# The output projection of a hybrid decoder layer as seven products of quarter matrices

## The chip, the core and the metric

The kernel runs on one core of a Trainium2 chip. The core has five engines, each with an instruction queue of its own that it works off in order: TensorE (PE) multiplies matrices, with weight loads (PEld) beside it; VectorE (DVE), ScalarE (ACT) and GpSimd (POOL) work elementwise; SyncE (SP) only starts transfers (DMA). The metric is device time in microseconds (us), the median of several runs of one program; the profile is of one more execution.

## What is computed

One layer: RMSNorm of `x`, one wide input projection, three branches (sparse attention `a`, sliding-window attention `b`, an RWKV-7 scan `c`), and then what matters here. Every array is float32; there are 1024 tokens of width 1024.

```python
y_a = y_a * jax.nn.silu(cols["a_z"])      # likewise y_b, y_c
gates = jax.nn.sigmoid(cols["merge"].reshape(b, t, N_BRANCHES, d) + b_merge[l])
mixed = (gates[:, :, 0] * (y_a @ proj_a[l])
         + gates[:, :, 1] * (y_b @ proj_b[l])
         + gates[:, :, 2] * (y_c @ proj_c[l]))
x = x + mixed @ w_out[l]
return rms_norm(x, final_g)
```

## The kernel before, in words

Every float32 matrix is split into a high part that the matmul takes without loss and a low remainder, so that a product costs three matmuls (`mm3`): high by high, high by low, low by high. A stationary operand of 128x128 is loaded, and 512 columns stream past it.

The program up to `finish` is the same before and after. `finish` has two stages.

**The product stage.** For branch 2, then 1, then 0 (`br`), and for each pair `m2` of the eight blocks of 128 output columns, the weights of the branch projection are loaded (`wr`) and split (`wh`, `wl`), the merge gates `g` are loaded from DRAM scratch, and four tiles of PSUM (`pp`, four buffers) are filled, each 128x512. A tile costs 6 matmuls in branches 2 and 1, and 12 in branch 0. DVE reads a tile out of PSUM and multiplies it by its gate: into `mixed` for branch 2, into a temporary `t` (three buffers) for the others, which POOL then adds to `mixed` (in the last step DVE does). In the text, branch 0's sixteen tiles are numbered 1 to 16 in their order; a tile can only be begun when the tile four before it has been read. The branch inputs `y` are loaded and split by `gated` a step or more ahead; the eight row blocks of `w_out` are loaded (`wor`) and split (`o_hi` by ACT, `o_lo` by DVE) in between, as the table `WO` says.

**The output stage.** For each of eight blocks `b` of 128 tokens: load `x`, split the block of `mixed` (`mh`, `ml`), two PSUM tiles `op` of 128x512 with 24 matmuls each (the last block's second tile is cut in two of 256 columns, each in a PSUM tile of its own), add to `x`, square and sum (ACT), multiply by `final_g` (POOL), scale by the root mean square, store.

Instructions are written in program order and a list scheduler then decides the order of each engine's queue, also of SP's; buffers are handed out from free ones. No engine looks past the head of its queue.

Of the kernel before, what the change touches and what calls it, by code (L numbers as in the profile page):

```python
# [1140 lines left out]
def finish(tc, a, out, eps, split_w, mm3, wst, y_scr, o_scr, z_scr, g_scr):  # L1141
    nc = tc.nc
    pe, act, dve, pool = nc.tensor, nc.scalar, nc.vector, nc.gpsimd
    KB = ((0, 4), (4, 2), (6, 2))

    GF, GL = (6, 7), {(2, 0): (4,), (2, 2): (5,), (2, 4): (0,), (2, 6): (1,), (1, 0): (2,), (1, 2): (3,)}
    HB_, GB, YB, TT_, OB = 5, 4, 14, 3, 1
    WO = {(1, 2): (4,), (1, 6): (5,), (0, 0): (6, 7), (0, 2): (0, 1), (0, 4): (2, 3)}
    with ExitStack() as st:
        wo = st.enter_context(tc.tile_pool(name="wo", bufs=1, side="right"))  # L1150
        mxp = st.enter_context(tc.tile_pool(name="mx", bufs=1, side="right"))
        mixed = mxp.tile([P, KT, T], F32, name="mixed")
# [4 lines left out]
        wk = yp = st.enter_context(tc.tile_pool(name="yy", bufs=YB))

        def parts(names, shape, first):

            return [(hp if first else yp).tile(shape, F32R, name=n, tag="ya" if first else "yy") for n in names]

        with tc.tile_pool(name="pp", bufs=4, space=PSUM) as pp:
# [22 lines left out]
            o_hi, o_lo = {}, {}  # L1186
            for br in (2, 1, 0):
                i0, n = KB[br]
                for m2 in range(0, 8, 2):
# [4 lines left out]
                    for h in range(2):
                        nc.sync.dma_start(gs[h], g_scr[br][m2 // 2][:, :, h * NH:(h + 1) * NH].rearrange("m p t -> p m t"))
                    for i in GL.get((br, m2), ()):
                        ys[i] = gated(i)
                    for k in WO.get((br, m2), ()):

                        if k < 4:  # L1200
                            o_hi[k], o_lo[k] = parts(("o_hi", "o_lo"), [P, D], k == 0)
                        else:
                            o_hi[k], o_lo[k] = [wo.tile([P, D], F32R, name=n, tag=f"wo{k}", bufs=2) for n in ("o_hi", "o_lo")]
                        raw = hp.tile([P, D], F32, name="wor", tag="wor", bufs=OB)
# [19 lines left out]
        nc.sync.dma_start(fg, a["final_g"].to_broadcast([P, D]))  # L1224
        for b in range(NB):
            bs = slice(b * P, (b + 1) * P)
            x = hp.tile([P, D], F32, name="x", tag="h", bufs=HB_)
            nc.sync.dma_start(x, a["x"][bs])
            sq = wk.tile([P, D], F32, name="sq", tag="g", bufs=GB)
            ss = wk.tile([P, 4], F32, name="ss", bufs=2)  # L1230
            mh, ml = [yp.tile([P, KT, P], F32R, name=n, tag="yy") for n in ("mh", "ml")]
            for ks in (slice(0, 6), slice(6, 8)):
                act.activation(mh[:, ks], mixed[:, ks, bs], AF.Copy, scale=0.5)
                dve.scalar_tensor_tensor(ml[:, ks], mixed[:, ks, bs], 0.5, mh[:, ks].bitcast(F32), op0=OP.mult,
                                         op1=OP.subtract)

            cuts = (0, 512, 768, 1024) if b == NB - 1 else (0, 512, 1024)
            for i, (n0, n1) in enumerate(zip(cuts, cuts[1:])):
                ns = slice(n0, n1)
                ps = po.tile([P, NH], F32, name="op")[:, 0:n1 - n0]  # L1240
                dense(mm3(ps, lambda k: (mh[:, k], ml[:, k]), lambda k: (o_hi[k][:, ns], o_lo[k][:, ns]), KT))
                dve.tensor_add(x[:, ns], x[:, ns], ps)
                act.activation(sq[:, ns], x[:, ns], AF.Square, accum_out=ss[:, i:i + 1])
                if i:
                    dve.tensor_add(ss[:, 0:1], ss[:, 0:1], ss[:, i:i + 1])
                pool.tensor_mul(x[:, ns], x[:, ns], fg[:, ns])
            act.activation(ss[:, 0:1], ss[:, 0:1], AF.Sqrt, bias=eps[:, 0:1], scale=1.0 / D)
            dve.reciprocal(ss[:, 0:1], ss[:, 0:1])
            act.activation(x[:, 0:NH], x[:, 0:NH], AF.Copy, scale=ss[:, 0:1])
            dve.tensor_scalar(x[:, NH:], x[:, NH:], ss[:, 0:1], None, op0=OP.mult)  # L1250
            nc.scalar.dma_start(out[bs, 0:NH], x[:, 0:NH])
            nc.sync.dma_start(out[bs, NH:], x[:, NH:])


# [43 lines left out]
```

## Time and profile before

| | us |
|---|---|
| median of three runs | 1163.83 |
| lowest and highest of them | 1160.35, 1166.82 |
| the profiled execution | 1166.12 |
| its span (first to last recorded instruction) | 1164.4 |

The span is what the rows below count in, from 0; the profiled execution's own time lies 1.7 us above its span, and 2.3 us above the median of the runs. PE is busy for 1127.4 us of the span, DVE for 732.6, ACT for 562.8 and POOL for 209.8. The product stage begins on PE at 980.1 us, branch 0 at 1027.1 us and the output stage at 1070.7 us.

### The profile page before, as it was taken

What the parts mean: (1) busy time and instruction counts of PE and PEld (TensorE: products, weight loads), DVE (VectorE), ACT (ScalarE), POOL (GpSimd) and SP (SyncE); (2) the same over time, 40 slices, a digit from 0 to 9 for tenths busy, and PEclk for the clock granted to TensorE, in tenths of its full rate; (3) what the DMA queues carried; (4) which work ended last, traced back from release to release, by engine and by line L of the source; (5) the groups of instructions that cost most, each with busy time, mean ns of one, the idle gap of its engine ahead of it and who ended that gap; (6) DMA issues with size and microseconds to landing.
All of it is one profiled execution on the core that took longest, in us unless ns stands there. A gap on an engine that the chain in (4) does not pass through costs nothing.

```text
span 1164.4 us, 18199 instructions
## 1 busy us (share of the span) xinstructions
PE 1127.4 (97%) x6838; PEld 925.2 (79%) x6838; DVE 732.6 (63%) x1468; ACT 562.8 (48%) x1311; POOL 209.8 (18%) x230
## 2 busy tenths in 40 slices
PE   6989999999999899989999999999999999999997
PEld 6868887678868898868778778887888778788886
DVE  6486725977337221794788787458878776676322
ACT  7544134724326222554677665457766654222322
POOL 1100000100013011181112111211111120373222
PEclk9989999999999999999999999999999999999999
DMA  6012411122402121111111111111111169882221
GB/s 236 17 42 65 118 60 37 55 91 82 124 20 82 67 93 37 46 49 55 48 47 41 51 50 47 45 55 42 48 48 42 41 226 308 277 286 79 73 73 55
DMA packets 61464, 97.73 MB, mean 84 GB/s; under 512 B 16192, under 2 KB 24768, under 8 KB 61120
## 3 DMA queue, kind: packets, MB, share of 16 engines
q1 hardware_dynamic: 59936, 94.31, 24.9%
q10 hardware_dynamic: 1440, 2.26, 0.5%
q8 instruction: 54, 0.88, 0.3%
q14 instruction: 34, 0.28, 0.1%
HBM read 69.81 MB, written 26.74 MB: 83 GB/s over the span
## 4 chain that ended last, share of the span: by engine, by line
PE 74%; DVE 12%; ACT 6%; DMA 5%; issue 2%; SPq 0%; POOLq 0%; POOL 0%; ACTq 0%; DVEq 0%
PE pj L214 12%; PE pj L218 12%; PE pj L216 12%; PE s L1035 4%; PE tr L877 3%; DVE p L1071 3%; PE op L216 2%; PE op L214 2%; PE op L218 2%; ACT p L1044 2%; PE pv L868 2%; PE pv L869 2%; PE pp L214 2%; PE pp L218 2%; PE pp L216 2%
## 5 line engine op out<-in xcount | busy, mean ns | idle before, releaser
L214 PE MATMUL pj<-x_hi,wh 128*128 128x512 f32 x768 | 306.6, 399 | 4.0 <-DVE xr L403 3.2
L218 PE MATMUL pj<-x_hi,wl 128*128 128x512 f32 x768 | 306.7, 400 | 1.4 <-DVE wl L197 1.4
L216 PE MATMUL pj<-x_lo,wh 128*128 128x512 f32 x768 | 306.7, 399 | 0.0
L214 PEld LDWEIGHTS pj<-x_hi,wh 128*128 128x128 f32 x768 | 145.6, 190 | 33.5 <-DVE xr L403 3.6
L218 PEld LDWEIGHTS pj<-x_hi,wl 128*128 128x128 f32 x768 | 145.7, 190 | 30.3 <-DVE wl L197 1.9
L216 PEld LDWEIGHTS pj<-x_lo,wh 128*128 128x128 f32 x768 | 145.6, 190 | 30.2 <-issue 1.9
L196 ACT ACTIVATE wh<-wr 128x512 fp32r<-128x512 f32 (+1 forms) x120 | 70.0, 600 | 119.2 <-PE pj L216 84.0
L1044 ACT ACTIVATE p<-s,nm 128x512 f32<-128x512 f32 (+3 forms) x160 | 93.4, 589 | 43.1 <-DVE nm L1041 23.6
L197 POOL TENSOR_TENSOR wl<-wr,wh 128x512 fp32r<-128x512 f32 x58 | 77.1, 1342 | 191.6 <-ACT wh L196 161.6
L881 DVE TENSOR_TENSOR tl<-tr,th 128x512 fp32r<-128x512 f32 x132 | 89.8, 684 | 19.5 <-ACT th L879 18.3
L879 ACT ACTIVATE th<-tr 128x512 fp32r<-128x512 f32 x132 | 78.7, 597 | 43.8 <-PE tr L877 42.1
L1041 DVE TENSOR_REDUCE nm<-s 128x1 f32<-128x512 f32 (+3 forms) x130 | 84.8, 660 | 22.2 <-PE s L850 18.3
L877 PE MATMUL tr<-ident,p 128*128 128x128 f32 x528 | 81.3, 275 | 4.7 <-DVE tl L881 3.5
L1035 PE MATMUL s<-k,q 128*128 128x512 f32 (+3 forms) x320 | 82.3, 354 | 0.2
L877 PEld LDWEIGHTS tr<-ident,p 128*128 128x128 f32 x528 | 62.8, 141 | 20.4 <-DVE tl L881 6.2
L197 DVE TENSOR_TENSOR wl<-wr,wh 128x512 fp32r<-128x512 f32 (+1 forms) x62 | 45.9, 749 | 47.0 <-ACT wh L196 43.3
L868 PE MATMUL pv<-th,V 128*128 128x512 f32 (+1 forms) x162 | 68.1, 426 | 2.5 <-DVE o L855 2.5
L1035 PEld LDWEIGHTS s<-k,q 128*128 128x128 f32 x320 | 54.2, 188 | 14.6 <-ACT p L1044 4.7
L1071 DVE TENSOR_SCALAR p<-p,nm 128x512 f32<-128x512 f32 (+3 forms) x160 | 62.8, 460 | 0.7
L869 PE MATMUL pv<-tl,V 128*128 128x512 f32 (+1 forms) x162 | 59.9, 376 | 0.0
L214 PE MATMUL pp<-y_hi,wh 128*128 128x512 f32 x128 | 50.3, 393 | 2.2 <-ACT wh L196 1.3
L216 PE MATMUL op<-o_lo,mh 128*128 128x512 f32 (+1 forms) x136 | 51.2, 377 | 0.0
(307 smaller groups left out, 2006.2 us busy)
## 6 DMA issues: line engine op xcount, KB each, us to landing
wr<-w SPq DMA_DIRECT2D x96, 256.0 KB, 2.8
g_scr<-gs SPq DMA_DIRECT2D x48, 256.0 KB, 2.0
g<-g_scr SPq DMA_DIRECT2D x24, 512.0 KB, 5.6
xr<-x SPq DMA_DIRECT2D x8, 512.0 KB, 5.5
z_scr<-gs SPq DMA_DIRECT2D x16, 256.0 KB, 2.2
wor<-w_out SPq DMA_DIRECT2D x8, 512.0 KB, 4.7
x<-x SPq DMA_DIRECT2D x8, 512.0 KB, 5.4
o_scr<-ol SPq DMA_DIRECT2D x24, 128.0 KB, 2.4
```

Of the source, the lines that this page charges most:

```text
L197: weng[0].tensor_sub(lo, raw, hi.bitcast(F32))
L214: pe.matmul(ps, lh, rh, start=k == 0, stop=False)
L216: pe.matmul(ps, lh, rl, start=False, stop=False)
L218: pe.matmul(ps, ll, rh, start=False, stop=k == n - 1)
L868: pe.matmul(pv, v.rearrange("p j d -> p (j d)"), th, start=start, stop=False, skip_group_check=True)
L869: pe.matmul(pv, v.rearrange("p j d -> p (j d)"), tl, start=False, stop=stop, skip_group_check=True)
L877: pe.transpose(tr[:, h], p4[h], ident)
L881: dve.tensor_sub(tl, tr, th.bitcast(F32))
L1035: pe.matmul(ps[:, i], q[h0 + i][:, qs], ks[j][:, kc:kc + n], start=i == 0 and j == 0, stop=wrap and j == 1, skip_group_check=True)
L1041: dve.tensor_reduce(nm[:, c, 0, hs], ps, axis=AX.X, op=OP.max, negate=True)
L1044: act.activation(weights(h, c), ps[:, i], AF.Exp, bias=nm[:, c, 0, h:h + 1], accum_out=nm[:, c, 1, h:h + 1])
L1071: eng.tensor_scalar(p, p, nm[:, c, 3, h:h + 1], None, op0=OP.mult)
```

## The change

The output projection becomes one level of Winograd's form of Strassen's method. `mixed` (tokens by inner dimension) and `w_out` (inner dimension by columns) are cut into 2x2 quarters A11..A22 and B11..B22 of 512x512. With S1 = A21+A22, S2 = S1-A11, S3 = A11-A21, S4 = A12-S2 and T1 = B12-B11, T2 = B22-T1, T3 = B22-B12, T4 = B21-T2, seven products replace eight: A11 B11, S1 T1, S2 T2, S4 B22, S3 T3, A12 B21, A22 T4. Two sets of four PSUM banks hold running sums: `op` (called u) takes A11 B11, then S2 T2, S3 T3 and A22 T4 on top, and is added to `x` after each; `pp` (called c) takes S1 T1 and S4 B22, and then A12 B21 anew.

The order of the loops is turned: products outside (`steps`), the four token blocks of a half inside. A unit is one product and one token block: 12 matmuls of 512 columns into one bank, and one add to half a row of `x` by DVE. All eight blocks of `x` stay on chip (five in the buffers `h`, three in `yy`). `rows` forms a unit's sum on POOL and splits it (ACT, DVE), three units ahead (`AHEAD`); `weigh` forms and splits one of four 128-row slices of a product's weights, in the step before the one that uses it, or for B11 and T1 inside branch 0; the four splits of A11 also stand inside branch 0 (at `m2 == 6` in the code). `done` squares, sums and scales what is final. The loads of quarters replace the loads of row blocks: B11 in branch 1, B12 and B22 in branch 0, B21 at the start of the output stage.

```diff
-    HB_, GB, YB, TT_, OB = 5, 4, 14, 3, 1
-    WO = {(1, 2): (4,), (1, 6): (5,), (0, 0): (6, 7), (0, 2): (0, 1), (0, 4): (2, 3)}
+    HB_, GB, YB, TT_ = 5, 4, 14, 3
...
+        def load(name, j, n, first=False):
+            raws[name] = []
+            for c in range(2):
+                t = (hp if first else yp).tile([P, 2, NH], F32, name="wor", tag="wor" if first else "yy")
+                k = 4 * j + 2 * c
+                nc.sync.dma_start(t, a["w_out"][k:k + 2, :, n * NH:(n + 1) * NH].rearrange("k p n -> p k n"))
+                raws[name] += [t[:, i] for i in range(2)]
...
+        def weigh(name, k, minus=None, into=None):
...
+            hi, lo = ws[name]
+            t = raws[name][k]
+            if minus:
+                pool.tensor_sub(t, raws[minus[0]][k], raws[minus[1]][k])
+            act.activation(hi[:, k], t, AF.Copy)
+            dve.tensor_sub(lo[:, k], t, hi[:, k].bitcast(F32))
...
+        def rows(what, i):
...
+            if what == "S1":
+                pool.tensor_add(src, a21, a22)
+            elif what == "S2":
+                pool.tensor_sub(src, src, a11)
+            elif what == "S3":
+                pool.tensor_sub(src, a11, a21)
+            elif what == "S4":
+                pool.tensor_sub(src, a12, src)
...
+            act.activation(t[:, 0], src, AF.Copy, scale=0.5)
+            dve.scalar_tensor_tensor(t[:, 1], src, 0.5, t[:, 0].bitcast(F32), op0=OP.mult, op1=OP.subtract)
+            return t
...
-                    for k in WO.get((br, m2), ()):
...
-                        nc.sync.dma_start(raw, a["w_out"][k])
-                        for h in range(2):
-                            ns = slice(h * NH, (h + 1) * NH)
-                            act.activation(o_hi[k][:, ns], raw[:, ns], AF.Copy)
-                            dve.tensor_sub(o_lo[k][:, ns], raw[:, ns], o_hi[k][:, ns].bitcast(F32))
+                    if br == 1 and m2 == 6:
+                        load("B11", 0, 0, True)
+                    if br == 0 and m2 == 0:
+                        load("B12", 0, 1)
+                        for k in range(4):
+                            weigh("B11", k)
+                    if br == 0 and m2 == 4:
+                        load("B22", 1, 1)
+                        for k in range(4):
+                            weigh("T1", k, ("B12", "B11"), "B11")
+                    if br == 0 and m2 == 6:
+                        ahead = [rows("A11", i) for i in range(4)]
...
-        for b in range(NB):
...
-            cuts = (0, 512, 768, 1024) if b == NB - 1 else (0, 512, 1024)
...
-                ps = po.tile([P, NH], F32, name="op")[:, 0:n1 - n0]
-                dense(mm3(ps, lambda k: (mh[:, k], ml[:, k]), lambda k: (o_hi[k][:, ns], o_lo[k][:, ns]), KT))
...
+            steps = (("A11", "B11", "+u", 0, 0, False, None),
+                     ("S1", "T1", "+c", 1, 1, False, ("T2", ("B22", "T1"), "T1")),
+                     ("S2", "T2", "u", 0, 1, False, ("B22", None, None)),
+                     ("S4", "B22", "c", 0, 1, True, ("T3", ("B22", "B12"), "B12")),
+                     ("S3", "T3", "u", 1, 1, True, ("B21", None, None)),
+                     ("A12", "B21", "+c", 0, 0, True, ("T4", ("B21", "T2"), "T2")),
+                     ("A22", "T4", "u", 1, 0, True, None))
...
+                for c0, c1 in ((0, 256), (256, 512)) if at == len(todo) - 1 else ((0, 512),):
+                    for k in range(4):
+                        pe.matmul(ps[:, c0:c1], t[:, 0, k], hi[:, k, c0:c1], start=new and k == 0, stop=False,
+                                  skip_group_check=True)
...
+                    x, o = xs[4 * half + i], col_ * NH
+                    dve.tensor_add(x[:, o + c0:o + c1], x[:, o + c0:o + c1], ps[:, c0:c1])
+                    if full:
+                        done(4 * half + i, o + c0, o + c1)
```

Since the scheduler places `weigh` and `rows` by what is ready, their place in the queues is not that of the code. Three places follow; a name's number tells buffers apart.

**POOL in branch 0.** `mixed<-mixed,t` is the add of one tile of branch 0 (`t_10150` to `t_10260` are tiles 3 to 8 before; `t_10120` to `t_10198` are tiles 2 to 6 after). `wor_10019` and `wor_10021` hold the two halves of B11, then T1, then T2; `wor_10077` and `wor_10079` hold B12, then T3; `wor_10247` and `wor_10249` hold B22. Before:

```order
L1223 TENSOR_TENSOR mixed_9554<-mixed_9554,t_10150 128x512
L1223 TENSOR_TENSOR mixed_9554<-mixed_9554,t_10166 128x512
L1223 TENSOR_TENSOR mixed_9554<-mixed_9554,t_10212 128x512
L1223 TENSOR_TENSOR mixed_9554<-mixed_9554,t_10228 128x512
L1223 TENSOR_TENSOR mixed_9554<-mixed_9554,t_10244 128x512
L1223 TENSOR_TENSOR mixed_9554<-mixed_9554,t_10260 128x512
```

After:

```order
L1191 TENSOR_TENSOR wor_10021<-wor_10079,wor_10021 128x512 x2
L1278 TENSOR_TENSOR mixed_9554<-mixed_9554,t_10120 128x512
L1278 TENSOR_TENSOR mixed_9554<-mixed_9554,t_10136 128x512
L1278 TENSOR_TENSOR mixed_9554<-mixed_9554,t_10152 128x512
L1191 TENSOR_TENSOR wor_10019<-wor_10247,wor_10019 128x512 x2
L1191 TENSOR_TENSOR wor_10077<-wor_10247,wor_10077 128x512
L1278 TENSOR_TENSOR mixed_9554<-mixed_9554,t_10182 128x512
L1191 TENSOR_TENSOR wor_10021<-wor_10249,wor_10021 128x512 x2
L1191 TENSOR_TENSOR wor_10077<-wor_10247,wor_10077 128x512
L1191 TENSOR_TENSOR wor_10079<-wor_10249,wor_10079 128x512 x2
L1278 TENSOR_TENSOR mixed_9554<-mixed_9554,t_10198 128x512
```

Between the adds of tiles 4 and 6 there now stand eight subtractions, four that form T2 and four that form T3; the first rows are the second half of T1.

**DVE in branch 0.** `t<-g,pp` reads a tile out of PSUM (`t_10166` to `t_10260` are tiles 4 to 8 before; `t_10152` to `t_10230` are tiles 4 to 8 after), `wl` is the low part of projection weights, `o_lo` that of `w_out`, and `mh<-mixed,mh` the low part of A11's rows. Before:

```order
L1221 SCALAR_TENSOR_TENSOR t_10166<-g_10086,pp_10153 128x512
L1209 TENSOR_TENSOR o_lo_10192<-wor_10193,o_hi_10191 128x512
L197 TENSOR_TENSOR wl_10264<-wr_10265,wh_10263 128x512
L197 TENSOR_TENSOR wl_10264<-wr_10269,wh_10263 128x512
L1221 SCALAR_TENSOR_TENSOR t_10212<-g_10179,pp_10199 128x512
L1221 SCALAR_TENSOR_TENSOR t_10228<-g_10179,pp_10215 128x512
L1209 TENSOR_TENSOR o_lo_10278<-wor_10279,o_hi_10277 128x512 x2
L1221 SCALAR_TENSOR_TENSOR t_10244<-g_10180,pp_10231 128x512
L1221 SCALAR_TENSOR_TENSOR t_10260<-g_10180,pp_10247 128x512
```

After:

```order
L1276 SCALAR_TENSOR_TENSOR t_10152<-g_10074,pp_10139 128x512
L198 TENSOR_TENSOR wl_10234<-wr_10235,wh_10233 128x512
L198 TENSOR_TENSOR wl_10234<-wr_10239,wh_10233 128x512
L1276 SCALAR_TENSOR_TENSOR t_10182<-g_10165,pp_10169 128x512
L1276 SCALAR_TENSOR_TENSOR t_10198<-g_10165,pp_10185 128x512
L1216 SCALAR_TENSOR_TENSOR mh_10343<-mixed_9554,mh_10343 128x512
L1216 SCALAR_TENSOR_TENSOR mh_10346<-mixed_9554,mh_10346 128x512
L1276 SCALAR_TENSOR_TENSOR t_10214<-g_10166,pp_10201 128x512
L1216 SCALAR_TENSOR_TENSOR mh_10349<-mixed_9554,mh_10349 128x512
L1216 SCALAR_TENSOR_TENSOR mh_10352<-mixed_9554,mh_10352 128x512
L1276 SCALAR_TENSOR_TENSOR t_10230<-g_10166,pp_10217 128x512
```

Two of the four splits of A11 now stand ahead of the read of tile 7 and two ahead of that of tile 8; each waits for ACT's high part, which waits for POOL's add of tile 6. The splits of `w_out` that stood between these reads are gone from this place.

**SP in branch 0.** `wr_10171` to `wr_10269` are the projection weights of steps `m2` = 2 and 4 before, `wr_10157` to `wr_10239` the same after; `g` are gates. Before:

```order
L195 DMA wr_10171<-proj 128x512
L195 DMA wr_10175<-proj 128x512
L1195 DMA g_10179<-g_scr01_92 128x2x512
L1205 DMA wor_10185<-w_out 128x1024
L1195 DMA g_10180<-g_scr01_92 128x2x512
L195 DMA wr_10265<-proj 128x512
L195 DMA wr_10269<-proj 128x512
L1228 DMA x_10656<-x 128x1024
L1205 DMA wor_10193<-w_out 128x1024
```

After:

```order
L196 DMA wr_10157<-proj 128x512
L196 DMA wr_10161<-proj 128x512
L1250 DMA g_10165<-g_scr01_92 128x2x512
L1250 DMA g_10166<-g_scr01_92 128x2x512
L196 DMA wr_10235<-proj 128x512
L196 DMA wr_10239<-proj 128x512
L1250 DMA g_10243<-g_scr02_93 128x2x512
L1177 DMA wor_10247<-w_out 128x2x512
L1177 DMA wor_10249<-w_out 128x2x512
L1250 DMA g_10244<-g_scr02_93 128x2x512
```

The two loads of B22 (`wor_10247`, `wor_10249`) stand behind `wr_10239`, which waits until its buffer has been read: by DVE's second `wl_10156`, the low part of step 2's weights. In DVE's queue that subtraction follows two `o_lo_10252<-wor_10019,o_hi_10251`, the first two low parts of T1.

## Rows read from the trace of the kernel before

**Rows 1.** The page: the span, and section 1 (busy time, share of span, instructions).

```profile
span 1164.4 us, 18199 instructions
PE 1127.4 (97%) x6838; PEld 925.2 (79%) x6838; DVE 732.6 (63%) x1468; ACT 562.8 (48%) x1311; POOL 209.8 (18%) x230
```

**Rows 2.** Stretches: start:end, length, busy (instructions) by engine, clock, DMA share, GB/s.

```profile
950.00:1000.00 50.00, 50.00 (x222) 41.30 (x222) 29.21 (x51) 19.32 (x37) 2.54 (x2) 1.00 0.84 280
1000.00:1050.00 50.00, 47.77 (x206) 38.03 (x206) 36.92 (x50) 11.69 (x23) 31.48 (x22) 1.00 0.85 279
1070.00:1158.00 88.00, 88.00 (x412) 73.83 (x411) 31.37 (x56) 26.95 (x61) 20.82 (x16) 1.00 0.17 60
```

**Rows 3.** Timeline of PE: output stage's first, first narrow, last; branch 0's first.

```profile
1070.72 0.39 PE L214 MATMUL op<-o_hi,mh 128*128 128x512 f32 x1
...
1152.32 0.28 PE L214 MATMUL op<-o_hi,mh 128*128 128x256 f32 x1
...
1157.95 0.28 PE L218 MATMUL op<-o_hi,ml 128*128 128x256 f32 x1
...
1027.09 0.47 PE L214 MATMUL pp<-y_hi,wh 128*128 128x512 f32 x1
```

**Rows 4.** Timeline of SP's queue and of DVE where attention ends.

```profile
932.60 0.80 SPq L1171 DMA_DIRECT2D y<-y_scr  x2
...
950.63 0.32 SPq L1175 DMA_DIRECT2D z<-z_scr  x1
...
952.09 0.42 DVE L982 TENSOR_TENSOR th<-tr,th 64x256 fp32r<-64x256 f32 x1 [0.44 <-ACT th L981]
```

**Rows 5.** Waits of PE from 975 us on: us in total, times, longest us.

```profile
PE pp L214 <- ACT wh L196: 1.3, 1, 1.3
PE pp L214 <- DVE t L1221: 0.5, 1, 0.5
PE pp L214 <- DVE mixed L1218: 0.4, 1, 0.4
```

**Rows 6.** Timeline of POOL; below, the page of tile t: ns min/median/max.

```profile
1016.98 16.41 POOL L1223 TENSOR_TENSOR mixed<-mixed,t 128x512 f32<-128x512 f32 x11 [1.23 <-DVE t L1221]
...
L1221 DVE SCALAR_TENSOR_TENSOR t<-g,pp x32: 673/680/689, 1006.9 to 1071.7; 128x512 f32<-128x512 f32 x32
L1223 POOL TENSOR_TENSOR mixed<-mixed,t x28: 1283/1296/1752, 1007.8 to 1061.9; 128x512 f32<-128x512 f32 x28
```

**Rows 7.** The page of tile wor: ns min/median/max, and time to landing.

```profile
L1208 ACT ACTIVATE o_hi<-wor x16: 613/618/634, 981.3 to 1055.5; 128x512 fp32r<-128x512 f32 x16
L1209 DVE TENSOR_TENSOR o_lo<-wor,o_hi x16: 678/688/1780, 986.7 to 1056.2; 128x512 fp32r<-128x512 f32 x16
...
DMA to landing us min/median/max: 3.4/4.7/7.5
```

**Rows 8.** Timeline of DVE among POOL's adds.

```profile
1020.51 1.19 DVE L1209 TENSOR_TENSOR o_lo<-wor,o_hi 128x512 fp32r<-128x512 f32 x1
...
1026.87 1.17 DVE L197 TENSOR_TENSOR wl<-wr,wh 128x512 fp32r<-128x512 f32 x1
```

**Rows 9.** Timeline of PE around a wait early in the program.

```profile
69.82 0.39 PE L218 MATMUL pj<-x_hi,wl 128*128 128x512 f32 x1
73.41 0.80 PE L214 MATMUL pj<-x_hi,wh 128*128 128x512 f32 x1 [3.20 <-DVE xr L403]
...
79.81 0.40 PE L214 MATMUL pj<-x_hi,wh 128*128 128x512 f32 x1
```

**Rows 10.** Stretches of the same place (columns as in rows 2).

```profile
76.00:77.00 1.00, 1.00 (x4) 0.71 (x4) 1.00 (x2) 0.00 (x0) 0.00 (x0) 0.50 0.00 0
80.00:81.00 1.00, 1.00 (x6) 0.78 (x5) 1.00 (x1) 0.00 (x0) 0.00 (x0) 1.00 0.14 18
```

**Rows 11.** Timeline of DVE and of ACT's queue behind the last matmul.

```profile
1158.27 0.42 DVE L1242 TENSOR_TENSOR x<-x,op 128x256 f32<-128x256 f32 x1 [1.72 <-PE op L218]
...
1160.78 0.34 ACTq L1251 DMA_DIRECT2D out<-x  x1
```

More of the change, by code (lines that the diff above doesn't have):

```diff
@@ L42 @@
 WR, WB = 512, 2
+AHEAD = 3
 G_0, WP, PSP = 0, 1, 0
@@ L1161, in parts @@
             return [(hp if first else yp).tile(shape, F32R, name=n, tag="ya" if first else "yy") for n in names]
+        raws = {}
+        def load(name, j, n, first=False):
[5 more added lines that the diff above has]
+                raws[name] += [t[:, i] for i in range(2)]
+        ws = {}
+        def weigh(name, k, minus=None, into=None):
+            if k == 0:
+                ws[name] = [wo.tile([P, 4, NH], F32R, name=n, bufs=2) for n in ("o_hi", "o_lo")]
+                if into:
+                    raws[name] = raws[into]
+            hi, lo = ws[name]
[4 more added lines that the diff above has]
+            dve.tensor_sub(lo[:, k], t, hi[:, k].bitcast(F32))
+        sums = []
+        def rows(what, i):
+            b1, b2 = slice(i * P, (i + 1) * P), slice((4 + i) * P, (5 + i) * P)
+            a11, a12, a21, a22 = mixed[:, 0:4, b1], mixed[:, 4:8, b1], mixed[:, 0:4, b2], mixed[:, 4:8, b2]
+            if what == "S1" and i % 2 == 0:
+                t = wk.tile([P, 2, 4, P], F32, name="s", tag="g", bufs=GB)
+                sums.extend(t[:, j] for j in range(2))
+            src = {"A11": a11, "A12": a12, "A22": a22, "S3": a21}.get(what) if what[0] == "A" or what == "S3" else sums[i]
+            if what == "S1":
[6 more added lines that the diff above has]
+                pool.tensor_sub(src, a12, src)
+            first = what == "A11" and i < 2
+            t = (hp if first else yp).tile([P, 2, 4, P], F32R, name="mh", tag="ya" if first else "yy")
+            act.activation(t[:, 0], src, AF.Copy, scale=0.5)
+            dve.scalar_tensor_tensor(t[:, 1], src, 0.5, t[:, 0].bitcast(F32), op0=OP.mult, op1=OP.subtract)
+            return t
         with tc.tile_pool(name="pp", bufs=4, space=PSUM) as pp:
@@ L1185, in finish @@
             ys = {i: gated(i) for i in GF}
-            o_hi, o_lo = {}, {}
             for br in (2, 1, 0):
@@ L1197, in finish @@
                         ys[i] = gated(i)
-                    for k in WO.get((br, m2), ()):
[L1200 to L1204, printed above, removed]
-                        nc.sync.dma_start(raw, a["w_out"][k])
-                        for h in range(2):
-                            ns = slice(h * NH, (h + 1) * NH)
-                            act.activation(o_hi[k][:, ns], raw[:, ns], AF.Copy)
-                            dve.tensor_sub(o_lo[k][:, ns], raw[:, ns], o_hi[k][:, ns].bitcast(F32))
+                    if br == 1 and m2 == 6:
[10 more added lines that the diff above has]
+                        ahead = [rows("A11", i) for i in range(4)]
                     last = br == 0 and m2 == 6
@@ L1223, in finish @@
                             eng.tensor_add(mx, mx, t)
-        nc.sync.dma_start(fg, a["final_g"].to_broadcast([P, D]))
-        for b in range(NB):
[L1226 to L1235, printed above, removed]
-            cuts = (0, 512, 768, 1024) if b == NB - 1 else (0, 512, 1024)
-            for i, (n0, n1) in enumerate(zip(cuts, cuts[1:])):
-                ns = slice(n0, n1)
-                ps = po.tile([P, NH], F32, name="op")[:, 0:n1 - n0]
-                dense(mm3(ps, lambda k: (mh[:, k], ml[:, k]), lambda k: (o_hi[k][:, ns], o_lo[k][:, ns]), KT))
[L1242 to L1252, printed above, removed]
@@ new lines, in finish, with done @@
+            nc.sync.dma_start(fg, a["final_g"].to_broadcast([P, D]))
+            xs, norms = [], []
+            for b in range(NB):
+                x = hp.tile([P, D], F32, name="x", tag="h", bufs=HB_) if b < HB_ else yp.tile([P, D], F32, name="x", tag="yy")
+                nc.sync.dma_start(x, a["x"][b * P:(b + 1) * P])
+                xs.append(x)
+                norms.append(hp.tile([P, 8], F32, name="ss", bufs=NB))
+            def done(b, c0, c1):
+                x, ss, cs = xs[b], norms[b], slice(c0, c1)
+                n = parts_done[b]
+                sq = wk.tile([P, 2, NH], F32, name="sq", tag="g", bufs=GB)[:, 0]
+                act.activation(sq[:, 0:c1 - c0], x[:, cs], AF.Square, accum_out=ss[:, n:n + 1])
+                if n:
+                    dve.tensor_add(ss[:, 0:1], ss[:, 0:1], ss[:, n:n + 1])
+                parts_done[b] += 1
+                width[b] += c1 - c0
+                pool.tensor_mul(x[:, cs], x[:, cs], fg[:, cs])
+                if width[b] == D:
+                    bs = slice(b * P, (b + 1) * P)
+                    act.activation(ss[:, 0:1], ss[:, 0:1], AF.Sqrt, bias=eps[:, 0:1], scale=1.0 / D)
+                    dve.reciprocal(ss[:, 0:1], ss[:, 0:1])
+                    act.activation(x[:, 0:NH], x[:, 0:NH], AF.Copy, scale=ss[:, 0:1])
+                    dve.tensor_scalar(x[:, NH:], x[:, NH:], ss[:, 0:1], None, op0=OP.mult)
+                    nc.scalar.dma_start(out[bs, 0:NH], x[:, 0:NH])
+                    nc.sync.dma_start(out[bs, NH:], x[:, NH:])
@@ new lines, in finish @@
+            parts_done, width = [0] * NB, [0] * NB
+            steps = (("A11", "B11", "+u", 0, 0, False, None),
[6 rows of a table added]
+            todo = [(n, i) for n in range(len(steps)) for i in range(4)]
+            banks = {}
+            for at, (n, i) in enumerate(todo):
+                what, wname, bank, half, col_, full, nxt = steps[n]
+                if n == 0 and i == 0:
+                    load("B21", 1, 0)
+                if nxt:
+                    weigh(nxt[0], i, nxt[1], nxt[2])
+                while len(ahead) < min(at + AHEAD, len(todo)):
+                    m, j = todo[len(ahead)]
+                    ahead.append(rows(steps[m][0], j))
+                t, (hi, lo) = ahead[at], ws[wname]
+                ahead[at] = None
+                new = bank[0] == "+"
+                if new:
+                    banks[bank[1], i] = (po if bank[1] == "u" else pp).tile([P, NH], F32, name="op" if bank[1] == "u" else "pp")
+                ps = banks[bank[-1], i]
+                for c0, c1 in ((0, 256), (256, 512)) if at == len(todo) - 1 else ((0, 512),):
+                    for k in range(4):
+                        pe.matmul(ps[:, c0:c1], t[:, 0, k], hi[:, k, c0:c1], start=new and k == 0, stop=False,
+                                  skip_group_check=True)
+                        pe.matmul(ps[:, c0:c1], t[:, 0, k], lo[:, k, c0:c1], start=False, stop=False,
+                                  skip_group_check=True)
+                        pe.matmul(ps[:, c0:c1], t[:, 1, k], hi[:, k, c0:c1], start=False, stop=k == 3,
+                                  skip_group_check=True)
+                    x, o = xs[4 * half + i], col_ * NH
+                    dve.tensor_add(x[:, o + c0:o + c1], x[:, o + c0:o + c1], ps[:, c0:c1])
+                    if full:
+                        done(4 * half + i, o + c0, o + c1)
```

## The prediction

> **What bounds the kernel now.** I read the page's engine table first: PE is busy for 97% of the span, the next engine for 63% [rows 1]. A share over the whole span says nothing of one stage, so next came the stretches: in 950 to 1000 us and in the output stage PE is busy for every microsecond, at a granted clock of 1.00 [rows 2]. But the stages differ in what stands close behind. In 950 to 1050 the DMA engines are busy at 0.84 to 0.85 and move 280 GB/s, and POOL works for 31.48 of 50 us; in the output stage DMA is at 0.17, and DVE, ACT and POOL are each under 32 of 88 us [rows 2]. The waits say how near the next bound is: from 975 us on PE waits only three times, 2.2 us in all, and never for the output stage's operands [rows 5]. So a matmul saved in the output stage is time saved, while work put into branch 0, where the change puts much of its own, has little room on POOL and DMA.
>
> **1. The matmuls of the output stage.** Before, 360 of 512 columns start between 1070.72 and 1152.32, 0.2267 us apart, and 48 of 256 columns follow, 5.63 us for 47 steps, 0.120 each [rows 3]: 81.6 + 5.8 = 87.4 us. After, seven products by four token blocks are 28 units of 12; 27 stay whole and the last is cut into 24 of 256: 324 x 0.2267 + 24 x 0.120 = 76.3. That is **-11.0**. It needs the sums to be ready in time. In this stage POOL now makes 16 sums of rows, 4 of T4 and 17 products with `final_g`, 37 x 1.296 = 48 us of the 76 [rows 6], with three units (8.2 us) of lead; ACT and DVE split 24 blocks of rows and 20 slices of weights at 0.62 and 0.69 us each [rows 7] beside what they did, also under 76. I cost these at nothing, covered by PE's 76 us; without the cover one unit's sum and splits would be 1.30 + 0.62 + 0.69 = 2.6 us.
>
> **2. Loads moved later.** Before, eight loads of `y` and `z` for the product stage are issued between 932.60 and 950.63; after, the first stands behind attention's last matmul, which needs DVE's `th` of 952.09 [rows 4]. At 128 x 1024 x 4 bytes they are 4.2 MB, moved into 952 to 1027. Out of this stretch go three loads of `x` (1.6 MB), and 0.5 MB of `w_out` (three row blocks before, the two halves of B11 after): net +2.1 MB, at 280 GB/s 7.5 us if nothing absorbs it. But DMA is idle for 0.16 of its time there [rows 2]: 0.16/0.84 x 280 GB/s x 75 us = 4.0 MB, so all of it could be absorbed. Between 0 and 7.5 I take **+2**: the room is twice the load, but it is spread over the stretch while the loads come at its head.
>
> **3. Branch 0, the chain that decides.** I walk it with durations of before. Branch 0 begins at 1027.09 and a tile takes 12 x 0.2267 = 2.72 us.
> - POOL does eleven adds in a row until 1033.39, 16.41/11 = 1.49 each [rows 6]. The first two subtractions of T1 queue behind: 1036.4. ACT's high part 0.62, DVE's low part beside a busy POOL 1.19 [rows 7, 8]: 1038.2.
> - On DVE the low parts of step 2's projection weights stand behind these. First `wl_10156`, 1.17 [rows 8]: 1039.4. Tile 5, due at 1027.09 + 4 x 2.72 = 1038.0, needs it: about 1.5 us of stall. Then a read of 0.68 [rows 6] and the second `wl_10156`: 1041.2.
> - SP's `wr_10239` waits for that, and B22 is behind it: four issues of some 0.4 [rows 4], until 1042.8, the first half of B22 at 1042.4. Landing takes 4.7 in the median [rows 7]: 1047.1.
> - POOL then does eight subtractions (T2, T3) and the adds of tiles 5 and 6 in the order shown, ten operations of 1.49: 1062.0.
> - Only now can A11 be split: ACT 0.62, two low parts on DVE 1.38, and behind them in DVE's queue the read of tile 7, 0.68: 1064.7. PE's tile 11 needs that read, for four PSUM buffers allow no more. It is due at 1054.3 + 1.5 = 1055.8: a stall of 8.9.
>
> With the 1.5 this is **+10.4**. Queued behind DVE's waiting low part are all reads of tiles, and PE waits for them; no matmul beside branch 0 can hide it, for PE's queue is in order and the output stage needs the same A11. The lower end: POOL without a backlog and B22 early. Then the ten operations start after the add of tile 4 (1038.0 + 0.68 + 1.30 = 1040.0) and take 1.296 each: 1053.0, read of tile 7 at 1055.6, tile 11 due at 1054.3: +1.3. The upper end: landing of 7.5 and 1.75 per operation [rows 6, 7]: 1049.9 + 17.5 + 2.7 = 1070.1, so 14.3 + 1.5 = +15.8. I stay with the middle, since 1.49 is the mean of POOL's own run in this place and 4.7 the median of the same loads.
>
> On the durations of POOL and DVE when both work, the rows show the low part of `w_out` between 678 and 1780 ns and POOL's add between 1283 and 1752 [rows 6, 7]. The Trainium skill, "SBUF — State Buffer", section "Who interferes with whom", says that a DVE instruction with two inputs in SBUF contends with a GpSimd instruction that reads SBUF, and that the one that issues first holds the shared ports while the other waits. The trace agrees so far as the low part at 1020.51, inside POOL's run, takes 1.19 us and not 0.688 [rows 8].
>
> **4. The clock after the stall.** After an early wait of 3.20 us, PE's fifteen starts from 73.41 to 79.81 took 6.40 us instead of 15 x 0.2267 = 3.40; the granted clock was 0.50, the lower of its two levels (1.2 GHz), at 76 and 1.00 again at 80 [rows 9, 10]. A stall of 8.9 is longer than that wait. I take **+3.0**; the lower end is 0, since PE is densely busy before this stall and the row is from a program's start.
>
> **5. The last unit.** Before, the two 256-column parts have PSUM tiles of their own; now they share one, and by the order the second part's first matmul waits for DVE's add of the first. DVE's last add begins 0.32 us after the last matmul's start and takes 0.42 [rows 3, 11]; the matmul would have followed 0.12 after: 0.62, plus the pass of two signals. **+1.0**, from 0.4 to 1.5.
>
> **6. The tail.** From the last matmul (1157.95) to the issue of the store (1160.78) it is 2.8 us [rows 3, 11], the same steps after. But token blocks now become final 2.72 us apart instead of 10.9, so another block's operation may stand ahead: one of 0.42 [rows 11], **+0.4**, from 0 to 1.5.
>
> **The sum.** -11.0 + 2 + 10.4 + 3.0 + 1.0 + 0.4 = **+5.8 us** on the profiled execution's 1166.1 (span 1164.4 and 1.7 around it): 1171.9. That execution lies 2.3 above the median of the runs, 1163.8, which is what is forecast: **1169.6**.
>
> **The rivals.**
> - *The stall is hidden (faster).* Place: POOL between the adds of tiles 4 and 6. If B22 is there when POOL reaches T2, the stall is the 1.3 of the lower end, too short for the clock: -11.0 + 2 + 1.3 + 1.0 + 0.4 = -6.3, 1157.5. It decides from where stall and clock together cost less than 7.6 (the rest of the sum). For it: POOL's subtractions need not be slower than 1.296, and a later start (part 2) gives POOL and SP time to catch up. Against it: B22's issue behind the weights that T1 holds up, and eleven adds that already ran back to back.
> - *Half the stall, no clock fall.* B22 a few microseconds earlier and POOL at 1.3: a stall of 5.5, -2.1 in all, 1161.7. For it: the waits of before are short, and PE's queue is dense until the stall.
> - *The longer stall.* POOL waits out a DVE operation of 0.68 at each of its ten: 1.296 + 0.68 = 1.98 instead of 1.49, +4.9, which gives 1174.5; landing at 7.5 instead of 4.7 would give +2.8 more. For it: durations of 1752 and 1780 [rows 6, 7]. Against it: while POOL does these, DVE has little to do in this chain. The Trainium skill's section named above is the rule behind this case.
> - *Fewer matmuls than thought saved:* excluded, the counts are in the code.
>
> **How the numbers follow.** Forecast, as walked, +2.5 to +10 (1166 to 1174): 0.55. Hidden stall, 1155 to 1160: 0.12. Half, 1160 to 1166: 0.15. Longer, 1172 to 1179, part 2's upper end with it: 0.18. A measurement here can tell about 0.5%, 5.8 us, from no change: faster means under 1158.0, slower over 1169.6. Faster is most of the hidden case: 0.09. Same is its rest, the half case and nearly half of the forecast: 0.43. Slower: 0.48. The range 1160 to 1176 leaves out the hidden case and the top of the longer one, some 2 in 10.
>
> **What the profile after would show.** Right: some 76 us of PE in the output stage plus about 1; in branch 0 one wait of 7 to 11 us before tile 11, ended by DVE's `t`, with DVE waiting for ACT's `mh`, ACT for POOL's `mixed`, and POOL's `wor` for a DMA from `w_out`; granted clock of 0.50 behind it; the last 256 columns after a wait for DVE's `x`. Wrong: no wait over 2 us in branch 0 (part 3); PE waiting for ACT's `wh` or DVE's `t` before 1027 by more than 5 us (part 2); waits for `mh` in the output stage (part 1's cover).

## The result, and the profile after

| | us |
|---|---|
| changed kernel, median of four runs | 1176.97 |
| lowest and highest of them | 1175.32, 1178.77 |
| the kernel before beside it, median of four | 1163.95 |
| ratio, with its 95% interval | 1.0110 (1.0092 to 1.0128) |
| the profiled execution, its span | 1175.32, 1173.6 |

The change makes the kernel slower: by the ratio 10.7 to 14.9 us, by the medians 13.0. The direction is the one forecast; the size, +5.8, is not, and 1176.97 lies just above the range of 1160 to 1176. The profiled execution is the quickest of the four.

The page of the changed kernel, span and engine table, to be held against [rows 1]:

```profile
span 1173.6 us, 18172 instructions
...
PE 1119.7 (95%) x6778; PEld 917.2 (78%) x6778; DVE 776.4 (66%) x1504; ACT 576.4 (49%) x1335; POOL 258.8 (22%) x262
```

PE is busy for 7.7 us less, in a span 9.2 us longer: it is idle for 16.9 us more. The waits of PE from 975 us on (total, times, longest) say where, against 2.2 us in [rows 5]:

```profile
PE pp L215 <- DVE t L1276: 8.1, 2, 7.2
PE op L1337 <- DVE x L1344: 5.8, 1, 5.8
PE pp L219 <- DVE wl L198: 4.3, 2, 3.7
```

The timeline of PE gives the stages: the product stage's first matmul, branch 0's first, the output stage's first, and the two sides of the wait in the last unit with the last matmul.

```profile
978.43 0.39 PE L215 MATMUL pp<-y_hi,wh 128*128 128x512 f32 x1
...
1029.60 0.39 PE L215 MATMUL pp<-y_hi,wh 128*128 128x512 f32 x1
...
1083.31 0.39 PE L1337 MATMUL op<-o_hi,mh 128*128 128x512 f32 x1
...
1158.07 0.28 PE L1341 MATMUL op<-o_hi,mh 128*128 128x256 f32 x1
1164.10 0.58 PE L1337 MATMUL op<-o_hi,mh 128*128 128x256 f32 x1 [5.75 <-DVE x L1344]
...
1166.61 0.41 PE L1341 MATMUL op<-o_hi,mh 128*128 128x256 f32 x1
```

| stage, from first to next first start | before | after | forecast | measured |
|---|---|---|---|---|
| branches 2 and 1 (part 2) | 47.0 | 51.2 | +2 | +4.2 |
| branch 0 (parts 3 and 4) | 43.6 | 53.7 | +13.4 | +10.1 |
| output stage, to the last matmul (1 and 5) | 87.2 | 83.3 | -10.0 | -3.9 |
| behind it (6) | 6.5 | 7.0 | +0.4 | +0.5 |

That is +10.9 in the stages; the spans differ by 9.2 only because this execution came to the product stage 1.7 us earlier, at 978.4, which is scatter: in the nine further profiles below the stage begins anywhere between 975.9 and 980.2. The other 2 us up to the 13.0 of the medians belong to executions of which there is no profile. The output stage is the row that is out of line. The loads of `y` begin late, as forecast, 19.7 us after those of before [rows 4]:

```profile
952.30 0.80 SPq L1227 DMA_DIRECT2D y<-y_scr  x2
```

The output stage as two windows (columns as in [rows 2]); the first ends where PE stops in the last unit:

```profile
1083.30:1158.30 75.00, 75.00 (x337) 62.21 (x335) 65.90 (x82) 37.59 (x76) 49.02 (x32) 1.00 0.14 53
1158.30:1166.80 8.50, 2.75 (x13) 2.63 (x12) 4.91 (x14) 5.30 (x15) 4.56 (x5) 0.65 0.50 185
```

In the first PE is busy for all of its 75.00 us at a clock of 1.00: 74.8 us from the first start to 1158.07, where 324 x 0.2267 + 12 x 0.120 = 74.9 were forecast. The saving is there in full. But DVE is busy for 65.90 of 75 us (before: 31.37 of 88 [rows 2]), and the second window is PE waiting for it.

**The chain in branch 0.** One timeline of five engines, from B22's issue to PE's tile 11:

```profile
1044.43 0.93 SPq L1177 DMA_DIRECT2D wor<-w_out  x2
...
1050.16 3.78 POOL L1191 TENSOR_TENSOR wor<-wor 128x512 f32<-128x512 f32 x3 [0.64 <-DMA wor<-w_out]
...
1055.14 6.20 POOL L1191 TENSOR_TENSOR wor<-wor 128x512 f32<-128x512 f32 x5
1061.30 1.26 POOL L1278 TENSOR_TENSOR mixed<-mixed,t 128x512 f32<-128x512 f32 x1
...
1062.60 2.19 ACT L1215 ACTIVATE mh<-mixed 128x512 fp32r<-128x512 f32 x4 [15.77 <-POOL mixed L1278]
...
1063.26 1.29 DVE L1216 SCALAR_TENSOR_TENSOR mh<-mixed,mh 128x512 fp32r<-128x512 f32 x2 [11.99 <-ACT mh L1215]
1064.47 0.68 DVE L1276 SCALAR_TENSOR_TENSOR t<-g,pp 128x512 f32<-128x512 f32 x1
...
1065.20 0.79 PE L215 MATMUL pp<-y_hi,wh 128*128 128x512 f32 x1 [7.20 <-DVE t L1276]
```

Every step of the walk is here: B22 issued behind T1's hold-up (1044.43) and there 5.7 us later, POOL's ten operations without a gap (1050.16 to 1062.56), ACT's high parts, DVE's two low parts ahead of the read of tile 7 (1064.47), and PE after 7.20 us of idleness. But B22 itself held POOL for 0.64 us only: until 1049.51 POOL was at the adds of tiles 3 and 4, which could begin no earlier than 1046.53, since DVE's reads of these tiles (1045.71) stood behind low parts of T1. T1's hold-up reached the ten operations by two ways at once, and the walk had one of them.

**The clock.** Windows of 1 us, two behind the wait of 7.20 us and one in the last unit:

```profile
1066.00:1067.00 1.00, 1.00 (x3) 0.78 (x3) 1.00 (x1) 0.00 (x0) 0.88 (x1) 0.50 0.00 0
1070.00:1071.00 1.00, 1.00 (x6) 0.82 (x5) 1.00 (x3) 0.00 (x0) 0.00 (x0) 1.00 0.84 193
1165.00:1166.00 1.00, 1.00 (x7) 1.00 (x7) 0.48 (x2) 0.84 (x5) 0.67 (x1) 0.50 0.99 371
```

The granted clock is 0.50, the lower of its two levels (1.2 GHz), and then 1.00 again. Eight starts are slow from 1065.20 to 1068.76, 3.6 us instead of 1.8, and as many behind the wait of 3.71 us (1017.44 to 1020.96, 3.5 us); in the last unit all twelve are.

**DVE in the output stage.** Groups of DVE's instructions from 1086 to 1146 us (busy, mean ns | idle before):

```profile
L1193 DVE TENSOR_TENSOR o_lo<-wor,o_hi 128x512 fp32r<-128x512 f32 x18 | 21.5, 1235 | 0.8 <-ACT o_hi L1192 0.7
L1216 DVE SCALAR_TENSOR_TENSOR mh<-s,mh 128x512 fp32r<-128x512 f32 x12 | 15.2, 1277 | 0.5 <-ACT mh L1215 0.2
L1216 DVE SCALAR_TENSOR_TENSOR mh<-mixed,mh 128x512 fp32r<-128x512 f32 x12 | 10.5, 905 | 0.0
L1344 DVE TENSOR_TENSOR x<-x,op 128x512 f32<-128x512 f32 x12 | 8.1, 678 | 2.5 <-PE op L1341 2.4
```

The low parts of weights and of sums take 1235 and 1277 ns in the mean; I had costed them at 690. (POOL's own sums take 1520 to 1739 ns there, not the 1296 of part 1.) The adds to `x`, with one operand in PSUM, keep their 678. DVE is late long before the last unit: its adds start 0.43 to 1.25 us after the start of their unit's last matmul in the first four units, and 3.2 to 8.6 us after it from the fifth unit on. And the end of the stage on DVE:

```profile
1160.59 0.67 DVE L1344 TENSOR_TENSOR x<-x,op 128x512 f32<-128x512 f32 x1
1162.05 0.16 DVE L1294 TENSOR_TENSOR ss<-ss 128x1 f32<-128x1 f32 x1 [0.79 <-ACT sq L1292]
1162.57 0.16 DVE L1301 RECIPROCAL ss<-ss 128x1 f32<-128x1 f32 x1 [0.36 <-ACT ss L1300]
1162.65 0.67 DVE L1344 TENSOR_TENSOR x<-x,op 128x512 f32<-128x512 f32 x1
...
1163.63 0.41 DVE L1344 TENSOR_TENSOR x<-x,op 128x256 f32<-128x256 f32 x1
...
1167.49 0.41 DVE L1344 TENSOR_TENSOR x<-x,op 128x256 f32<-128x256 f32 x1
```

The last unit's first part has its last matmul at 1158.07, but the add that reads it starts at 1163.63, where 0.32 us behind was forecast: DVE is 5 us late, and between two adds it also waits for ACT's steps of finished blocks (0.79 and 0.36 us). The second part's matmuls, at 1164.10, need that add.

### The profile page after: what moved, and what is told of

It is laid out like the page before. It is cut to its first block, busy times and chain, and to the rows that moved or that the text cites. A ratio compares the mean times of both kernels' runs of the same rounds, so it can differ in the third digit from the quotient of the medians.

```text
span 1173.6 us, 18172 instructions
## 1 busy us (share of the span) xinstructions
PE 1119.7 (95%) x6778; PEld 917.2 (78%) x6778; DVE 776.4 (66%) x1504; ACT 576.4 (49%) x1335; POOL 258.8 (22%) x262
## 5 line engine op out<-in xcount | busy, mean ns | idle before, releaser
L972 POOL TENSOR_TENSOR p<-p,nm 128x256 f32<-128x256 f32 x16 | 10.3, 644 | 214.1 <-DVE nm L969 160.7
```

## The experiments

Each ran on one chip beside the kernel before. "Against the changed kernel" is the difference of the two ratios to the kernel before, times 1164 us; each ratio's interval is about 0.2% to either side, so such a difference is uncertain by some 3 us.

**e1: the last unit whole.**

```diff
-                for c0, c1 in ((0, 256), (256, 512)) if at == len(todo) - 1 else ((0, 512),):
+                for c0, c1 in ((0, 512),):
```

> The last unit stays one tile of 512 columns, so no matmul waits for DVE's add of a first part. Theory A (DVE runs about 6 us late at the end of the output stage, and the shared bank only shows it): PE's 5.75 us wait goes, but DVE's last add still begins near where the first part's add began (1163.6 of a 1173.6 us span), and the chain behind a 512-wide add is some 7 us, so the end moves by -2 to -4 us. Rival B (the shared bank itself costs the 6.9 us, DVE is in time otherwise): -6 to -7 us.

Ratio 1.0076 (1.0051 to 1.0100), 4.0 us less. PE's last matmul and DVE's last add:

```profile
1163.05 0.39 PE L1341 MATMUL op<-o_hi,mh 128*128 128x512 f32 x1
...
1169.15 0.68 DVE L1344 TENSOR_TENSOR x<-x,op 128x512 f32<-128x512 f32 x1
```

PE is done at 1163.05, 75.9 us after the stage's start (1087.12), so the 7 us of wait and slow clock are gone; but the add comes 6 us later all the same, and from the last matmul to the end it is 13.0 us instead of 7.0. Stage and end together take 88.9 us in this profile, against 90.3. This is theory A: the shared bank shows DVE's lateness and does not make it.

**e2: the splits of A11 behind the reads.**

```diff
-                    if br == 0 and m2 == 6:
-                        ahead = [rows("A11", i) for i in range(4)]
...
+            with tc.issue_after(MARK['act']), tc.issue_after(MARK['dve']):
+                ahead = [rows("A11", i) for i in range(4)]
```

`issue_after` queues what follows behind the named instruction of the same engine: here the read of tile 12 on DVE and the last split of projection weights on ACT.

> The four splits of A11 are queued on DVE behind the read of tile 12 and on ACT behind the last split of projection weights; POOL's order is unchanged. Theory A (tile 11 waits because DVE's read of tile 7 stands behind A11's low parts): the wait of 7.2 us before tile 11 and the clock of 0.50 behind it go, no wait over 1 us in branch 0 takes its place, -8 to -10 us. Rival B (POOL's run of ten operations is itself the bound: three buffers of t let the reads go only three tiles past POOL's last add): a wait of 3 to 7 us shows before tile 13 instead, and the time falls by less than 5 us.

Ratio 1.0044 (1.0025 to 1.0063), 7.7 us less. Timeline of DVE and PE:

```profile
1064.18 0.69 DVE L1275 SCALAR_TENSOR_TENSOR t<-g,pp 128x512 f32<-128x512 f32 x1 [4.92 <-POOL mixed L1278]
...
1065.01 0.47 PE L216 MATMUL pp<-y_hi,wh 128*128 128x512 f32 x1 [1.25 <-DVE t L1275]
```

The wait of 7.20 and the slow clock are gone, and branch 0 takes 45.2 us instead of 53.7. What is left of rival B: DVE's reads now wait for POOL's adds through the buffers of `t` (4.92 us idle on DVE), and 1.25 us of that reach PE before tile 13. This is theory A, with a remainder of B.

**e3: T2 and T3 behind the adds of branch 0.**

```diff
+                if name in ("T2", "T3"):
+                    with tc.issue_after(held[-1]):
+                        pool.tensor_sub(t, raws[minus[0]][k], raws[minus[1]][k])
```

> The eight subtractions of T2 and T3 are queued on POOL behind the last add of branch 0. Theory A (they delay the add of tile 6 and with it A11): the wait before tile 11 falls under 1 us, the clock stays at 1.00 there, -8 to -10 us. Rival B (the work only moves: POOL now makes eight subtractions right before the first sums of rows, and the second product waits for them): a wait of 2 to 6 us appears in the output stage and the time falls by 3 to 7 us.

Ratio 1.0042 (1.0024 to 1.0060), 7.9 us less. Branch 0 takes 43.5 us, as before the change, with no wait. On POOL the eight subtractions now stand ahead of the sums of rows:

```profile
1068.40 11.84 POOL L1194 TENSOR_TENSOR wor<-wor 128x512 f32<-128x512 f32 x8
1080.20 5.93 POOL L1211 TENSOR_TENSOR s<-mixed 128x512 f32<-128x512 f32 x4
```

The output stage then has two waits of 1.0 and 0.4 us for low parts, and still 6.4 in the last unit. So what held tile 11 was POOL's run between the adds; a small part of it comes back later, as B said.

**e4: without the sums of the output stage.**

```diff
-            if minus:
+            if minus and name != "T4":
...
-            if what == "S1":
-                pool.tensor_add(src, a21, a22)
```

> Left out: the sixteen sums of rows and the four subtractions of T4, on POOL; products take unsummed operands. Theory A (DVE's low parts in the output stage take 1.1 to 1.8 us instead of 0.68 because POOL works beside them, and so DVE falls behind): the low parts take about 0.7 us, DVE's adds follow their unit within 1.5 us, the wait in the last unit is under 1.5 us instead of 5.75, -5 to -7 us. Rival B (DVE is late by the number of its operations and by the square root and scale chains of finished blocks): the wait stays at 4 us or more and the time falls by under 2 us.

The kernel leaves out these sums, so its products are not those of the layer; what counts is the time. Ratio 1.0058 (1.0036 to 1.0079), 6.1 us less, all in the output stage (branch 0 keeps its 7.6 us wait). DVE's groups from 1086 to 1146 us, and PE's wait in the last unit:

```profile
L1208 DVE SCALAR_TENSOR_TENSOR mh<-mixed,mh 128x512 fp32r<-128x512 f32 x24 | 18.5, 797 | 0.0
L1193 DVE TENSOR_TENSOR o_lo<-wor,o_hi 128x512 fp32r<-128x512 f32 x20 | 14.5, 760 | 0.6 <-ACT o_hi L1192 0.6
L1336 DVE TENSOR_TENSOR x<-x,op 128x512 f32<-128x512 f32 x12 | 8.2, 683 | 8.4 <-PE op L1333 8.4
```

```profile
PE op L1329 <- DVE x L1336: 0.5, 1, 0.5
```

With POOL's sums gone the same low parts take 797 and 760 ns, and the adds wait for PE (8.4 us idle) instead of PE for them. DVE has the same operations as in the changed kernel, so their number is not the cause; nor did it wait for the sums there, since its idle time in those 60 us was under 4 us (0.8, 0.5 and 2.5 above). Its adds to the 27 whole units now start 0.43 to 2.7 us after the start of the unit's last matmul. This is theory A.

**e5: the sums on DVE.**

```diff
-                pool.tensor_sub(t, raws[minus[0]][k], raws[minus[1]][k])
+                dve.tensor_sub(t, raws[minus[0]][k], raws[minus[1]][k])
...
-                pool.tensor_add(src, a21, a22)
+                dve.tensor_add(src, a21, a22)
```

> All 28 subtractions and sums (T1 to T4, S1 to S4) go from POOL to DVE; POOL keeps the adds of branches 1 and 0 and the products with final_g. Theory A (both losses come from POOL: its run of ten operations holds back A11, and its work beside DVE makes DVE's low parts 1.1 to 1.8 us): the wait before tile 11 falls under 1 us, DVE's low parts in the output stage take about 0.7 us, the wait in the last unit is under 2 us; against the changed kernel -12 to -16 us. Rival B (DVE is what lacks time: it gets 28 x 0.68 = 19 us more): new waits of 2 to 5 us for DVE in branch 0 or at the second product, the last wait stays above 4 us, -4 to -9 us.

Ratio 1.0009 (0.9997 to 1.0022), 11.8 us less. PE's waits:

```profile
PE pp L219 <- DVE wl L198: 3.7, 1, 3.7
PE pp L215 <- DVE t L1276: 2.8, 3, 1.3
PE op L1337 <- DVE x L1344: 1.1, 1, 1.1
```

The edit moves 32 operations, 16 subtractions for T1 to T4 and 16 for the rows (the expectation counted 28). DVE does them and is nearly in time: its adds to the whole units start 0.43 to 3.9 us after the unit's last matmul, and PE waits 1.1 us in the last unit and 1.1 at most in branch 0. This is theory A, though 11.8 us is just under its 12. The group of 3.7 is the one before branch 0, which this edit does not touch.

**e6: the loads of `y` as early as before.** The buffers that were added to the pool `hp` go to a pool behind the others, so that `y` and `z` lie where attention no longer writes; the first `y` is issued at 930.38.

```diff
+        wop = st.enter_context(tc.tile_pool(name="wop", bufs=2))
...
-                t = (hp if first else yp).tile([P, 2, NH], F32, name="wor", tag="wor" if first else "yy")
+                t = (wop if first else yp).tile([P, 2, NH], F32, name="wor", tag="wor" if first else "yy")
```

> The two first raw halves of w_out and the sums of squares get a pool of their own behind the others, so the inputs of the product stage lie at the addresses that they had before and their loads start before attention ends, as they did; the loads of x and of quarters move forward too. Theory A (the later loads cause the waits of 0.94 and 3.71 us before 1020 and the clock of 0.50 behind them, and B22's late landing at 1050.16 is the head of the chain to tile 11): the first two go, -4 to -6 us, and the wait before tile 11 falls to under 3 us with a clock of 1.00, in all -10 to -14 us; the end of the output stage stays as it is. Rival B (DMA's throughput, not the start of the loads, is the bound there): the waits before branch 0 stay within 2 us of what they are, -0 to -3 us.

Ratio 1.0011 (0.9997 to 1.0025), 11.5 us less. PE's waits, and POOL among the adds of branch 0:

```profile
PE op L1338 <- DVE x L1345: 5.5, 1, 5.5
PE pp L215 <- DVE t L1277: 3.0, 2, 2.8
```

```profile
1034.46 5.04 POOL L1192 TENSOR_TENSOR wor<-wor 128x512 f32<-128x512 f32 x4
1039.45 1.75 POOL L1279 TENSOR_TENSOR mixed<-mixed,t 128x512 f32<-128x512 f32 x1
1041.16 2.99 POOL L1192 TENSOR_TENSOR wor<-wor 128x512 f32<-128x512 f32 x2
```

B22 is there when POOL comes to T2, so the eight subtractions spread between the adds and tile 11 does not wait at all: branch 0 takes 44.2 us. B12 and T1 come earlier too, so the run does not separate B22's landing from T1's hold-up. Before branch 0 the wait of 3.71 is gone; one of 2.80 for a read of DVE's stays. This is theory A for the chain; for branches 2 and 1 it is half of it (49.1 us, against 51.2 and 47.0).

**e7 and e8: the edits of e5 and e6 together, then with e1's too.**

> The last two edits together: sums on DVE and the loads of y as early as before. If the losses are the three that the trace shows (late loads about 6 us, A11 behind POOL's run about 9 us, DVE late in the last unit about 7 us), 18 to 22 us go against the changed kernel, and it is 5 to 9 us faster than the kernel before, 11 less what the shared bank and the tail leave. If the gains overlap or DVE becomes the bound, it comes out within 3 us of the kernel before.

Ratio 0.9946 (0.9927 to 0.9964), 1157.4 us: 19.1 us less than the changed kernel, where 18 to 22 were expected if the three losses add up, and 6.3 us less than the kernel before.

> Sums on DVE and early loads, and the last unit not cut. Theory A (with the shared bank the cut only puts DVE's second add and a second chain behind the first): PE's wait of 1.1 us goes and the part from the last matmul to the end grows by less than it saves, 1 to 2.5 us faster than with the cut (1157.4), so 1155 to 1156.5. Rival B (the cut still pays, since with DVE nearly in time the chain behind the last add is shorter for 256 columns): 0.5 to 1.5 us slower than with the cut.

Ratio 0.9921 (0.9900 to 0.9942), median 1155.1 against 1164.4 for the kernel before beside it: 7 to 12 us faster than before, the quickest version tried. PE's waits from 975 us on:

```profile
PE pp L215 <- DVE t L1277: 3.0, 2, 1.7
PE pp L215 <- ACT o_hi L1193: 0.9, 1, 0.9
```

None is in the output stage, which takes 75.9 us to its last matmul. Behind that it is 8.4 us, 1.9 more than before. In e7 the two are 77.5 and 8.1, so leaving the unit whole is worth 1.3 us in the profiles, as theory A has it; the times, 2.9 us apart by the ratios, do not settle it by themselves.

**e9: the kernel before, with the late loads alone.**

```diff
-    HB_, GB, YB, TT_, OB = 5, 4, 14, 3, 1
+    HB_, GB, YB, TT_, OB = 5, 4, 14, 3, 2
```

> The kernel before with a second buffer for the raw row blocks of w_out and nothing else: it moves the inputs of the product stage to addresses that attention still uses, so that their loads start behind attention's last matmul, as in the changed kernel, with the old output projection. Theory A (the late loads are enough for the waits ahead of branch 0): waits of 3 to 5 us between 1000 and 1025 with a clock of 0.50 behind them, 3 to 6 us slower than before. Rival B (the loads of quarters and their splits cause these waits): within 1.5 us of the kernel before.

Ratio 1.0079 (1.0056 to 1.0102), 6.5 to 11.9 us slower. The first `y` is issued behind attention, and PE waits three times from 975 us on:

```profile
949.76 0.80 SPq L1171 DMA_DIRECT2D y<-y_scr  x2
```

```profile
PE pp L214 <- ACT wh L196: 2.5, 1, 2.5
PE pp L218 <- DVE wl L197: 2.3, 1, 2.3
PE pp L214 <- DVE t L1221: 2.0, 1, 2.0
```

The product stage takes 98.5 us instead of 90.6, the output stage 87.2 as before. Rival B is out: one more buffer of 4 KB per partition in the old kernel brings such waits without any quarter. Two of them, 4.5 us together, end at 1011.8 and 1014.6, where theory A put them; the third, 2.28 us, ends at 1029.8 in branch 0, where it had none, and the whole is above its 3 to 6 us. With two slow stretches of some 1.5 us each, and less the 2.2 us of waits before, they make 7.6 of the 7.9 us. Why branch 0 waits for `wl` longer here than in the changed kernel (0.6) was not separated.

## Why the prediction came out wrong

**What failed is part 5, and under it a sentence of part 1.** Part 5 priced the wait in the last unit at +1.0, at most 1.5, from a DVE that takes up the first part's add as soon as it is there. Measured: 6.03 us from start to start instead of 0.12, and the eleven steps behind it, at the low clock, take 2.51 us instead of 1.32: 5.9 + 1.2 = 7.1. The premise failed in part 1: "I cost these at nothing", with DVE's splits at 0.69. Beside POOL's sums they take 1.24 to 1.28, the twelve whose rows lie in `mixed` (S3, A12, A22) 0.91 (e4: 0.76 to 0.80 without): 20 x 0.55 + 12 x 0.59 + 12 x 0.22 = 21 us more, and DVE has 66 of 75 us full. PE feels it only in the last unit: elsewhere a bank is needed again only eight units on, with seven units or 19 us in between, and no add starts more than 8.6 us behind. I had the rows for it, 1780 and 1.19 [rows 7, 8], and used them in branch 0 alone.

**Part 1's -11.0** was right: 74.9 us forecast and 74.8 measured to the end of the first part.

**Part 2, +2** was mis-sized within its bounds: +4.2, of which 3.71 + 0.94 are waits and 1.7 the clock behind them, less the 2.2 us of waits that were there before. e9 shows that a late start of the loads is enough for such waits; in e6 the early start takes back 2.1 of the 4.2, and what causes the rest was not separated.

**Part 3, +10.4, and part 4, +3.0**: the mechanism was right (e2 and e3 each break one link, e6 its head), and the size nearly, in part by luck. The read of tile 7 was forecast to end at 1064.7 and ended at 1065.15; but POOL's ten operations began 3.1 us later than forecast, at 1050.16, and took 12.4 us instead of 14.9, and these errors nearly cancel. As branch 0 had begun 2.5 us later, the stall was 7.4 instead of 8.9. The wait for `wl_10156` before tile 5 was 0.6, not 1.5. The clock cost 1.7, not 3.0.

**Part 6, +0.4**: +0.5.

So the sum of +5.8 lacks 6.1 in part 5 and 2.2 in part 2, and has 3.3 too much in parts 3 and 4. No case had DVE as the late engine of the output stage. The rival with a DVE operation waited out at each of POOL's steps covers the measured time, but not its cause: it was set in branch 0, where POOL's ten took 1.24 us each while DVE had nothing to do; the engines slowed each other in the output stage, and there DVE's lateness is what PE met.

The Trainium skill, "SBUF — State Buffer", section "Who interferes with whom", says that a DVE instruction with two inputs in SBUF contends with GpSimd's reads and that one with at most one, outside its two-port modes, does not. The trace agrees on both: 1235 and 1277 ns for the low parts, 678 and 675 for the adds that read PSUM.

## What to carry to other kernels

Cost an engine's added operations at the duration that they have beside the other engine that the same change loads, and ask how late each queue ends, not only whether its busy time fits under PE's: lateness that PE never meets in the middle comes out at the first shared buffer or at the end. Ask of sums that replace matmuls whether they slow the splits beside them: here 32 more operations on DVE were cheaper than the same on POOL. And look at what a new buffer in a pool does to the addresses behind it: 4 KB moved the start of 4 MB of loads.

## What the runs showed of the hardware that was not expected

After waits of 3.71 and 7.20 us PE ran at the lower clock for eight starts, 1.7 us lost each time, and not for the fifteen of [rows 9], whose wait was 3.20: the length of the wait did not set the length of the slow stretch. Waits of 1.25 us in e2 and 1.1 us in e5, in branch 0 and in the last unit, left the spacing at 0.23 and 0.12 from the second or third start on. In e9 the slow stretch did not begin at the wait: behind 2.28 us of waiting PE made five starts 0.22 to 0.34 apart, and only from 1031.38 on were they 0.43 apart (granted clock 0.56 from 1031 to 1032).
